# A macaron decoder trunk on one core: chunk of four feature tiles first, and the pair by seven block products, in feed-forwards 2 to 4

## The chip, the cores and the metric

One core of one Trainium2 chip runs the kernel. The metric is device microseconds of one execution; the time is the median of several. The engines: TensorE (PE) multiplies and transposes, VectorE (DVE), ScalarE (ACT) and GpSimd (POOL) work on elements, SyncE (SP) issues loads.

## The reference

Two layers on x of 512 tokens by 1024 features, float32. Each is a feed-forward, a token mixer and a feed-forward, all on a residual stream:

```python
def swiglu(x, w_in, w_out):
    g, u = jnp.split(x @ w_in, 2, axis=-1)
    return (jax.nn.silu(g) * u) @ w_out

for i in range(DEPTH):
    h = h + 0.5 * swiglu(rms_norm(h, ffn1_norm[i]), ffn1_w_in[i], ffn1_w_out[i])
    hn = rms_norm(h, mix_norm[i])
    # layer 0: a gated linear recurrence; layer 1: a chunked causal spatial gate
    h = h + mixer(hn)
    h = h + 0.5 * swiglu(rms_norm(h, ffn2_norm[i]), ffn2_w_in[i], ffn2_w_out[i])
return rms_norm(h, final_norm)
```

D_FF is 2816, so w_in is 1024 x 5632 and w_out 2816 x 1024. There are four feed-forwards; "feed-forward 1" to "4" below are these in order of time.

## The kernel before

**Numbers.** All large products are float32 by three matmuls: each operand is split into a high and a low part (`hi`, `lo`; for weights `whi`, `wlo`), and high x high, low x high and high x low are summed. ACT writes the high part by a copy, VectorE the low part by a subtraction. A weight tile holds 128 x 1024 numbers and is split whole.

**Seven products.** `seven` multiplies a 2 x 2 block matrix (two halves of the tokens by two halves of the contracted features) with a 2 x 2 block matrix of weights by seven block products in place of eight, in the order P1, P2, P5, P6, P3, P7, Q4. Their left operands are A11, A12, S1, S2, S4, S3 and A22, where S1 = A21 - A22, S2 = S1 - A11, S4 = S2 + A12 and S3 = -S2 - A22. The weight sums are made in place in the raw weight tile, either by VectorE (`raw<-raw,raw`) or by an accumulating load that POOL issues. `cuts` divides the contracted tiles of a half; with two cuts each product takes two steps.

**Feed-forward.** `FF_PARTS` divides the 22 feature tiles into three parts. Each part projects in, applies SiLU and the product, transposes the result into left operands, and projects out (`out_blocks`). Part one is a pair of feature tiles and a chunk of four; parts two and three are two chunks of four. A chunk is `chunk`: `seven` with 512 columns and two cuts, 14 steps of 12 matmuls. The pair is `pair_plain`: four weight tiles (gate and up columns side by side, 512 columns), used in six steps of 12, 12, 24, 24, 12 and 12 matmuls, with A12, then A11 and S1 together, then A22 against the summed weights.

**Order of the work.** `manual_schedule` keeps the order written. The list `subs` holds all steps. In iteration i of the main loop each engine's queue gets, in this order: the hooks "pre", a weight add for step i+4, the split of the weights of step i+3, the hooks "mid" and "rest", loads, the matmuls of step i with what reads their banks, the hooks "end" and "late". There are four buffers for each of `whi` and `wlo`, so step i+3 is split into the buffers of step i-1. There are eight raw buffers (`rawp`).

**The norm between stages.** `BlockNorm` turns the residual X into the left operands of the next stage while the out-projection before it still runs. `quarter` is called when a quarter of X is final; the last is A21, at step n of that out-projection, and `rest(n)` sets the later sums and splits relative to n: `s2` in step n+4+i for column group i, its split in n+5+i, `s4` and `s3` in steps n4 and n3, their splits one later. So the next stage's first step is n+1. The flag `plain` serves the spatial block, whose second half also reads A21 itself. `BlockNorm` is made at four places: after the recurrent block (for feed-forward 2), after feed-forward 2 (for 3), after feed-forward 3 (for the spatial block, with `plain`), and after the spatial block (for 4).

Of the kernel before, what the change touches and what calls it, by code (L numbers as in the profile page):

```python
# [13 lines left out]
P = 128  # L14
# [3 lines left out]
DFF = 2816  # L18
# [6 lines left out]
V_F1, V_MIX, V_F2, V_CW, V_CB, V_GA, V_GX, V_LAM, V_SB = 0, 16, 32, 48, 80, 88, 96, 104, 112  # L25
# [2 lines left out]


FF_PARTS = (("p", 4), (4, 4), (4, 4))  # L30

RAW_BUFS = 8
SPLIT_AHEAD = 3
# [19 lines left out]
def trunk(ctx: ExitStack, tc: tile.TileContext, a: dict, out: bass.AP):  # L53
# [57 lines left out]
    class Raw:  # L111
# [4 lines left out]
        def __init__(self, src, shape, plus=None):  # L116
            self.src, self.shape, self.plus, self.uses, self.done = src, shape, plus, 0, 0
# [87 lines left out]
    subs = []  # L205
    hooks = {}

    def hook(n, phase, fn):


        hooks.setdefault((n, phase), []).append(fn)
# [106 lines left out]
    def seven(block, cuts, left, w, posts, order=None, own=False, apart=False, joined=None):  # L318

        bk, raw, held = {}, {}, []
        banks = dict(BANK, Q4=("Q", True)) if apart else BANK

        def mm_of(prod, ci):
            name, fresh = banks[prod]
            pairs = cuts[ci]  # L330

            def mm(sub):
                if fresh and ci == 0:
                    for s in range(2):
                        bk[name, s] = bank(name)[:, :w]
                if prod == joined and ci == 0:
                    held.extend((sub, q, i) for q, i in enumerate(pairs))
                    return
                for s in range(2):
                    ps = bk[name, s]  # L340
                    k = {} if fresh else dict(skip_group_check=True)
                    for sb, q, i in (held if prod == joined else []) + [(sub, q, i) for q, i in enumerate(pairs)]:
                        zh, zl = left(prod, i, s)
                        wh, wl = sb.hi[:, q, :], sb.lo[:, q, :]
                        end = i == cuts[-1][-1]
                        nc.tensor.matmul(ps, zh, wh, start=fresh and i == 0, stop=False, **k)  # L346
                        nc.tensor.matmul(ps, zl, wh, start=False, stop=False, **k)  # L347
                        nc.tensor.matmul(ps, zh, wl, start=False, stop=end, **k)  # L348
                    if ci == len(cuts) - 1 and prod in posts:
                        posts[prod](s, ps)  # L350
            return mm

        order = order or [(p, ci) for p in ORDER for ci in range(len(cuts))]
        for prod, ci in order:
            def new(k, n, plus=None):
                b = lambda k, n: block(k, n, cuts[ci])
                return raw_of(b(k, n), [P, len(cuts[ci]), w], plus and b(*plus))

            tile = then = tile_then = None
            if prod == "P1":  # L360
                r = raw[11, ci] = new(0, 0)
            elif prod == "P2":
                r = new(1, 0)
            elif prod == "P5":
                if own:
                    raw[11, ci] = new(0, 0, (0, 1))
                    if joined:
                        then = block(1, 1, cuts[ci])
                else:
                    tile = raw[12, ci] = new(0, 1)  # L370
                    tile_then = block(1, 1, cuts[ci])
                r = raw[11, ci]
            elif prod == "P6" and joined:
                r, then = raw[11, ci], block(1, 0, cuts[ci])
            elif prod == "P6":
                r, tile, then = raw[11, ci], new(1, 1), block(1, 0, cuts[ci])
                raw[22, ci] = tile
            elif prod == "P3":
                r = new(1, 1) if joined else raw[22, ci]
            elif prod == "P7":  # L380
                r = new(0, 1, (1, 1)) if own else raw[12, ci]
            else:
                r = raw[11, ci]
            subs.append(Sub(r, mm_of(prod, ci), None, tile, then, tile_then))
        return order
# [49 lines left out]
    class BlockNorm:  # L435


        def __init__(self, grow, plain=False):
            self.g = [Group(2), Group(2)]
            self.grow, self.plain = grow, plain  # L440

        def src(self, i, name):
            t0, c = QUARTER[name]
# [13 lines left out]
        def rest(self, n, a22=4):  # L457

            for i, g in enumerate(self.g):
                if a22 is not None:  # L460
                    hook(n + (9 if self.plain else a22), "mid", lambda g=g: g.parts("A22"))
                hook(n + 4 + i, "pre", g.s2)
                hook(n + 5 + i, "mid", lambda g=g: g.parts("S2"))
                n4, n3 = (n + 6 + i, n + 8 + i) if self.plain else (n + 7 + 2 * i, n + 10 + i)
                hook(n4, "pre", g.s4)
                hook(n4 + 1, "mid", lambda g=g: g.parts("S4", True))
                if self.plain:
                    hook(n3, "pre", lambda g=g: tt(g.new("A21"), g.f["S1"], g.f["A22"], ALU.add))
                    hook(n3 + 2, "mid", lambda g=g: g.parts("A21", True))
                hook(n3, "pre", g.s3)  # L470
                hook(n3 + 1, "mid", lambda g=g: (g.parts("S3", True), g.f.pop("S2")))
                hook(n3 + 1, "late", lambda g=g: g.f.pop("A22"))
# [148 lines left out]
    def in_block(w, col, cw):  # L621

        def block(k, n, cut):
            r0 = k * 512 + cut[0] * P
            return w[r0 : r0 + len(cut) * P, col(n) : col(n) + cw].rearrange("(q p) c -> p q c", p=P)
        return block

    def x_left():
        return left_of(lambda: S.z)


    def chunk(w_in, f0, nt, group):

        w = nt * P
        c1, c2, c3, c5, ht = {}, {}, {}, {}, {}

        def rt(t):
            return S.rt[:, t : t + 1]

        def new(d, s, name):  # L640
            d[s] = slot(name=name)[:, :w]
            return d[s]

        def p1(s, ps):
            act(new(c1, s, "c1"), ps, AF.Copy)

        def p2(s, ps):
            tt(c1[s], c1[s], ps, ALU.add)
            hook(now[0] + 1, "mid", lambda: act(c1[s], c1[s], AF.Silu, scale=rt(s)))

        def p5(s, ps):
            act(new(c5, s, "c5"), ps, AF.Copy)

        def p6(s, ps):
            act(new(c2, s, "c2"), ps, AF.Copy)

        def p3(s, ps):
            tt(c2[s], ps, c2[s], ALU.subtract)
            stt(c2[s], c2[s], rt(s), c1[s], ALU.mult, ALU.mult)
            ht[s] = c2[s]  # L660
            if s == 1:
                left_blocks(group, ht, 0)

        def p7(s, ps):
            act(new(c3, s, "c3"), ps, AF.Copy)
            hook(now[0] + 1, "mid", lambda: tt(c5[s], c5[s], c3[s], ALU.subtract))

        def q4(s, ps):
            s4 = slot(name="s4")[:, :w]
            act(s4, ps, AF.Silu, scale=rt(2 + s))  # L670
            stt(c5[s], c5[s], rt(2 + s), s4, ALU.mult, ALU.mult)
            ht[2 + s] = c5[s]
            if s == 1:
                left_blocks(group, ht, 1)

        seven(in_block(w_in, lambda n: n * DFF + f0 * P, w), [[0, 1], [2, 3]], x_left(), w,
              dict(P1=p1, P2=p2, P5=p5, P6=p6, P3=p3, P7=p7, Q4=q4))

    def pair_plain(w_in, f0, group, first=False):
# [58 lines left out]

    def ffn(w_in, w_out, norm):
        f0 = 0  # L740
        for i, sizes in enumerate(FF_PARTS):
            groups, p0 = [], f0
            for n in sizes:
                if n == "p":
                    groups.append(Group(1))
                    pair_plain(w_in, f0, groups[-1], not subs)
                    f0 += 2
                else:
                    groups.append(Group(n // 2))
                    chunk(w_in, f0, n, groups[-1])  # L750
                    f0 += n
            gs = out_blocks(w_out, p0, [g.n for g in groups], 0.5, norm if i == len(FF_PARTS) - 1 else None, own=True)
            gs.update(enumerate(groups))
# [533 lines left out]

    last = FinalNorm()
    ffn(a["ffn1_w_in"][0], a["ffn1_w_out"][0], TileNorm(V_MIX))
    recurrent(a["rec_w_in"][0], a["rec_w_out"][0], BlockNorm(V_F2))  # L1290
    ffn(a["ffn2_w_in"][0], a["ffn2_w_out"][0], BlockNorm(V_F1 + 8))
    ffn(a["ffn1_w_in"][1], a["ffn1_w_out"][1], BlockNorm(V_MIX + 8, True))
    spatial(a["sg_w_in"][0], a["sg_w_out"][0], BlockNorm(V_F2 + 8))
    ffn(a["ffn2_w_in"][1], a["ffn2_w_out"][1], last)
    hook(len(subs) - 24, "late", last.load)
    hook(len(subs) - 16, "rest", last.halve)
# [152 lines left out]
```

## Time and profile before

| | |
|---|---|
| median of 3 runs | 1651.8 us (1651.05 to 1652.23) |
| profiled execution, its span | 1651.2 us, 20805 instructions |
| granted TensorE clock, mean | 0.997 |
| loaded from memory | 269.55 MB, 165 GB/s over the span |

The page times one execution; its span is from the first instruction to the last. A group row gives the line, engine, operation, operands by name (buffer numbers left out) and shape, the count, then busy time and mean ns of one, then idle time of the engine just before and what ended it. A waits row gives who waited for whom: total us, times, longest. A timeline row gives start, duration, engine, line, operation, operands, and in brackets an idle time ahead of it with its releaser. A windows row gives a stretch, its length, then busy us and instructions of PE, PEld (weight load), DVE, ACT and POOL (or of those asked for), then the granted clock, DMA share and GB/s. Names: `p` are the pair's banks, A, B, C, Q those of `seven`, `r` the recurrent projection's, `a` and `s` hold left operands, `c` the chunk's results, `e` transposes.

### The profile page before, as it was taken

What the parts mean: (1) busy time and instruction counts of PE and PEld (TensorE: products, weight loads), DVE (VectorE), ACT (ScalarE), POOL (GpSimd) and SP (SyncE); (2) the same over time, 40 slices, a digit from 0 to 9 for tenths busy, and PEclk for the clock granted to TensorE, in tenths of its full rate; (3) what the DMA queues carried; (4) which work ended last, traced back from release to release, by engine and by line L of the source; (5) the groups of instructions that cost most, each with busy time, mean ns of one, the idle gap of its engine ahead of it and who ended that gap; (6) DMA issues with size and microseconds to landing.
All of it is one profiled execution on the core that took longest, in us unless ns stands there. A gap on an engine that the chain in (4) does not pass through costs nothing. (4 is left out here: it accounts for less than half of the span.)

```text
span 1651.2 us, 20805 instructions
## 1 busy us (share of the span) xinstructions
PE 1621.7 (98%) x7475; PEld 1333.0 (81%) x7475; DVE 1369.8 (83%) x1814; ACT 1035.8 (63%) x1490; POOL 212.3 (13%) x193
## 2 busy tenths in 40 slices
PE   8999999989999999999999999999999999999997
PEld 6788888878878888888888888888888888888885
DVE  5898897787798897878988978878966988879777
ACT  6656656666957656556676565566864765665655
POOL 1111111200010111111101111111100011121120
PEclk9999999999999999999999999999999999999999
DMA  6767876952463876876838778768863557686693
GB/s 205 159 171 176 209 163 153 219 141 77 102 153 92 189 169 162 218 177 157 202 95 181 176 162 209 184 163 204 216 169 90 151 122 186 166 208 169 157 230 79
DMA packets 161288, 273.02 MB, mean 165 GB/s; under 512 B 11312, under 2 KB 37536, under 8 KB 161184
## 3 DMA queue, kind: packets, MB, share of 16 engines
q1 hardware_dynamic: 113856, 182.74, 35.9%
q0 software_dynamic: 45536, 87.10, 31.4%
q10 hardware_dynamic: 1792, 1.84, 0.4%
q8 instruction: 59, 0.97, 0.2%
q14 instruction: 45, 0.37, 0.1%
HBM read 269.55 MB, written 2.10 MB: 165 GB/s over the span
## 5 line engine op out<-in xcount | busy, mean ns | idle before, releaser
L96 ACT ACTIVATE whi<-raw 128x1024 fp32r<-128x1024 f32 (+1 forms) x539 | 556.4, 1034 | 423.0 <-PE A L347 108.2
L87 DVE TENSOR_TENSOR wlo<-raw,whi 128x1024 fp32r<-128x1024 f32 (+1 forms) x539 | 641.0, 1192 | 203.7 <-ACT whi L96 202.8
L346 PE MATMUL A<-whi,hi 128*128 128x512 f32 x984 | 393.1, 399 | 4.3 <-DVE x L93 4.3
L347 PE MATMUL A<-whi,lo 128*128 128x512 f32 x984 | 386.2, 392 | 3.6 <-DVE lo L87 3.5
L348 PE MATMUL A<-wlo,hi 128*128 128x512 f32 x984 | 385.7, 392 | 0.2 <-DVE wlo L87 0.2
L347 PEld LDWEIGHTS A<-whi,lo 128*128 128x128 f32 x984 | 185.7, 189 | 43.8 <-DVE lo L87 7.1
L346 PEld LDWEIGHTS A<-whi,hi 128*128 128x128 f32 x984 | 185.5, 189 | 41.2 <-issue 4.7
L348 PEld LDWEIGHTS A<-wlo,hi 128*128 128x128 f32 x984 | 185.6, 189 | 40.8 <-DVE wlo L87 0.6
L347 PE MATMUL C<-whi,lo 128*128 128x512 f32 x544 | 212.4, 390 | 0.9 <-DVE lo L87 0.7
L346 PE MATMUL C<-whi,hi 128*128 128x512 f32 x544 | 212.4, 390 | 0.0
L348 PE MATMUL C<-wlo,hi 128*128 128x512 f32 x544 | 211.8, 389 | 0.0
L136 POOL DMA_DIRECT2D raw<-in_ffn_w_in_dram x80 | 96.4, 1205 | 757.3 <-DVE raw L87 551.8
L87 DVE TENSOR_TENSOR raw<-raw,raw 128x1024 f32<-128x1024 f32 (+1 forms) x116 | 139.1, 1200 | 0.5
L87 DVE TENSOR_TENSOR lo<-a,hi 128x512 fp32r<-128x512 f32 (+1 forms) x196 | 127.9, 659 | 11.5 <-ACT hi L96 11.1
L136 POOL DMA_DIRECT2D raw<-in_ffn_w_out_dram x74 | 85.5, 1162 | 382.8 <-DVE wlo L87 128.1
L96 ACT ACTIVATE hi<-a 128x512 fp32r<-128x512 f32 (+1 forms) x196 | 117.5, 601 | 8.4 <-DVE a L87 6.1
L347 PEld LDWEIGHTS C<-whi,lo 128*128 128x128 f32 x544 | 102.1, 188 | 24.2 <-DVE lo L87 3.3
L346 PEld LDWEIGHTS C<-whi,hi 128*128 128x128 f32 x544 | 102.1, 188 | 21.5 <-ACT c L96 0.4
L348 PEld LDWEIGHTS C<-wlo,hi 128*128 128x128 f32 x544 | 102.1, 188 | 21.1
L96 ACT ACTIVATE c<-A 128x512 f32<-128x512 f32 x126 | 74.1, 595 | 56.9 <-PE A L348 56.5
L346 PE MATMUL B<-whi,hi 128*128 128x512 f32 x272 | 109.1, 401 | 0.0
L348 PE MATMUL B<-wlo,hi 128*128 128x512 f32 x272 | 106.2, 391 | 0.0
(169 smaller groups left out, 2182.3 us busy)
## 6 DMA issues: line engine op xcount, KB each, us to landing
raw<-in_ffn_w_in_dram SPq DMA_DIRECT2D x160, 512.0 KB, 4.4
raw<-in_ffn_w_out_dram SPq DMA_DIRECT2D x100, 512.0 KB, 5.4
raw<-in_ffn_w_in_dram POOLq DMA_DIRECT2D x80, 512.0 KB, 7.6
raw<-in_ffn_w_out_dram POOLq DMA_DIRECT2D x62, 512.0 KB, 8.3
raw<-in_sg_w_in_dram SPq DMA_DIRECT2D x18, 512.0 KB, 5.1
raw<-in_rec_w_in_dram SPq DMA_DIRECT2D x16, 512.0 KB, 3.8
raw<-in_ffn_w_in_dram SPq DMA_DIRECT2D x30, 256.0 KB, 3.6
raw<-in_ffn_w_out_dram SPq DMA_DIRECT2D x20, 256.0 KB, 4.5
```

Of the source, the lines that this page charges most:

```text
L87: nc.vector.tensor_tensor(out=o, in0=x, in1=y, op=op)
L96: nc.scalar.activation(out=o, in_=x, func=f, **k)
L136: nc.gpsimd.dma_start(out=self.v, in_=src, accum_op=ALU.add)
L346: nc.tensor.matmul(ps, zh, wh, start=fresh and i == 0, stop=False, **k)
L347: nc.tensor.matmul(ps, zl, wh, start=False, stop=False, **k)
L348: nc.tensor.matmul(ps, zh, wl, start=False, stop=end, **k)
```

## The change

Feed-forwards 2 to 4 take `LATER_PARTS`: in part one the chunk of four tiles comes first and the pair second, and the pair is now `chunk` with two feature tiles: `seven` with 256 columns and one cut of four contracted tiles, seven steps of 24 matmuls. Feed-forward 1 keeps its parts. `BlockNorm` gets a flag `block`, which is set for the norms ahead of feed-forwards 2, 3 and 4 and, through `plain or block`, for the one ahead of the spatial block. The times of S4 and S3 that went by `plain` go by `block`, and so does the late split of A22, which now comes in n+9 for the first column group and n+10 for the second, in place of n+9 for both. `plain` alone still decides whether A21 itself is made.

```diff
+LATER_PARTS = ((4, 2), (4, 4), (4, 4))
...
-        def __init__(self, grow, plain=False):
+        def __init__(self, grow, plain=False, block=False):
             self.g = [Group(2), Group(2)]
-            self.grow, self.plain = grow, plain
+            self.grow, self.plain, self.block = grow, plain, plain or block
...
             for i, g in enumerate(self.g):
                 if a22 is not None:
-                    hook(n + (9 if self.plain else a22), "mid", lambda g=g: g.parts("A22"))
+                    hook(n + (9 + i if self.block else a22), "mid", lambda g=g: g.parts("A22"))
                 hook(n + 4 + i, "pre", g.s2)
                 hook(n + 5 + i, "mid", lambda g=g: g.parts("S2"))
-                n4, n3 = (n + 6 + i, n + 8 + i) if self.plain else (n + 7 + 2 * i, n + 10 + i)
+                n4, n3 = (n + 6 + i, n + 8 + i) if self.block else (n + 7 + 2 * i, n + 10 + i)
                 hook(n4, "pre", g.s4)
                 hook(n4 + 1, "mid", lambda g=g: g.parts("S4", True))
                 if self.plain:
...
-        seven(in_block(w_in, lambda n: n * DFF + f0 * P, w), [[0, 1], [2, 3]], x_left(), w,
+        cuts = [[0, 1], [2, 3]] if nt == 4 else [[0, 1, 2, 3]]
+        seven(in_block(w_in, lambda n: n * DFF + f0 * P, w), cuts, x_left(), w,
...
-        for i, sizes in enumerate(FF_PARTS):
+        for i, sizes in enumerate(FF_PARTS if not subs else LATER_PARTS):
...
-    recurrent(a["rec_w_in"][0], a["rec_w_out"][0], BlockNorm(V_F2))
-    ffn(a["ffn2_w_in"][0], a["ffn2_w_out"][0], BlockNorm(V_F1 + 8))
+    recurrent(a["rec_w_in"][0], a["rec_w_out"][0], BlockNorm(V_F2, block=True))
+    ffn(a["ffn2_w_in"][0], a["ffn2_w_out"][0], BlockNorm(V_F1 + 8, block=True))
     ffn(a["ffn1_w_in"][1], a["ffn1_w_out"][1], BlockNorm(V_MIX + 8, True))
-    spatial(a["sg_w_in"][0], a["sg_w_out"][0], BlockNorm(V_F2 + 8))
+    spatial(a["sg_w_in"][0], a["sg_w_out"][0], BlockNorm(V_F2 + 8, block=True))
```

## The prediction

> **What bounds the kernel now.** I read the page's engine table first, then TensorE's timeline, the busy time of each engine by stage, and the waits.
>
> ```profile
> PE 1621.7 (98%) x7475; PEld 1333.0 (81%) x7475; DVE 1369.8 (83%) x1814; ACT 1035.8 (63%) x1490; POOL 212.3 (13%) x193
> ```
>
> TensorE (PE) is the bound and VectorE (DVE) is next. PE's 98% is no price, because matmuls overlap; what one costs is read from start to start.
>
> ```profile
> 850.53 0.39 PE L700 MATMUL p<-whi,hi 128*128 128x512 f32 x1
> ...
> 855.97 0.39 PE L700 MATMUL p<-whi,hi 128*128 128x512 f32 x1
> ...
> 367.03 0.28 PE L219 MATMUL r<-zl,whi 128*128 128x256 f32 x1
> ...
> 374.23 0.28 PE L219 MATMUL r<-zl,whi 128*128 128x256 f32 x1
> ```
>
> The first two rows are 24 matmuls of 512 columns apart (the pair's fourth step): 5.44/24 = 0.227 us each. The other two are 60 matmuls of 256 columns apart (recurrent projection): 7.20/60 = 0.120 us. A step (one `Sub`: one product on one weight tile) of 12 wide matmuls is therefore 2.72 us.
>
> ```profile
> 506.01:529.04 23.03, 23.03 (x109) 18.98 (x108) 18.45 (x32) 15.22 (x24) 0.00 (x0) 1.00 0.29 92
> 529.04:569.03 39.99, 39.99 (x186) 32.92 (x184) 34.61 (x47) 26.79 (x40) 6.92 (x6) 1.00 0.76 163
> 569.03:599.29 30.26, 30.09 (x136) 24.27 (x134) 28.75 (x43) 17.26 (x26) 4.21 (x4) 1.00 0.77 202
> ```
>
> These are windows over feed-forward 2's pair, its chunk and its first out-projection: length, then busy PE, weight load, DVE, ACT, POOL. Together 93.3 us, of which VectorE works 18.45 + 34.61 + 28.75 = 81.8. It is hidden, but barely: 4.6, 5.4 and 1.5 us are spare.
>
> ```profile
> ACT whi L96 <- PE A L347: 108.2, 92, 1.9
> DVE wlo L87 <- ACT whi L96: 202.8, 171, 5.0
> PE A L347 <- DVE lo L87: 3.5, 3, 2.2
> ```
>
> The waits show the loop: ACT's weight split waits for PE (four split buffers, split three steps ahead, so the split for step k+3 starts when step k-1 ends), VectorE follows ACT, and PE hardly ever waits for a split operand.
>
> **The change part by part.**
>
> *Pair, PE.* Plain accumulation is 96 matmuls of 512 columns: 96 x 0.227 = 21.8 us. Seven products are 7 x 24 = 168 of 256: 168 x 0.120 = 20.2 us. That saves 1.6 us in each of three feed-forwards, **-4.8**. It is time of the bound itself, so it counts whole. The transposes stay the same in number. Bounds: -7.7 and +30, from the two rivals on spacing below; the 60-matmul row is the very shape with its weight loads, so I take it.
>
> *Chunk first: what is late next.* The pair asked for S1 in its third step; now S1 is read in step 5, a slack that buys nothing. S2, read in step 7 (P6, first cut), is next. Counted from the stage's first step, `block` puts S2's sums in steps 4 and 5 and its splits in 5 and 6 (as before), S4's splits in 7 and 8, S3's in 9 and 10, A22's in 9 and 10.
>
> ```profile
> 838.53:861.56 23.03, 22.64 (x96) 17.77 (x96) 0.88 (x3) 1.31 (x3) 1.00 0.29 92
> ...
> 849.36 0.68 DVE L87 TENSOR_TENSOR a<-s,a 128x512 f32<-128x512 f32 x1
> ...
> 516.86 0.68 DVE L87 TENSOR_TENSOR a<-s,a 128x512 f32<-128x512 f32 x1
> ...
> 1318.49 0.68 DVE L87 TENSOR_TENSOR a<-s,a 128x512 f32<-128x512 f32 x1
> ```
>
> The window is feed-forward 3's pair alone, 96 matmuls from 838.53. The sum of S2 starts 10.8 us into it, and likewise 10.85 after the 506.01 of the window of feed-forward 2; feed-forward 4 has its own at 1318.49. Ahead of it VectorE already does the adds for steps 5 and 6. What the items cost there, from start to start, shows in a stretch of the spatial in-projection, which works in this same order:
>
> ```profile
> 1182.89 1.22 DVE L87 TENSOR_TENSOR raw<-raw,raw 128x1024 f32<-128x1024 f32 x1
> 1184.02 1.22 DVE L87 TENSOR_TENSOR wlo<-raw,whi 128x1024 fp32r<-128x1024 f32 x1
> 1185.16 1.28 DVE L87 TENSOR_TENSOR c<-c,B 128x512 f32<-128x512 f32 x2
> 1186.35 0.68 DVE L87 TENSOR_TENSOR a<-s,a 128x512 f32<-128x512 f32 x1
> 1186.96 1.22 DVE L87 TENSOR_TENSOR wlo<-raw,whi 128x1024 fp32r<-128x1024 f32 x1
> 1188.09 0.68 DVE L87 TENSOR_TENSOR lo<-a,hi 128x512 fp32r<-128x512 f32 x1
> ...
> 1188.47 0.39 PE L346 MATMUL A<-whi,hi 128*128 128x512 f32 x1
> 1188.83 0.50 PE L347 MATMUL A<-whi,lo 128*128 128x512 f32 x1
> ```
>
> VectorE has no gap here: an add takes 1.13, a wlo 1.14, a 512-wide item 0.60. S2's lo, from 1188.09, makes step 7's second matmul start 0.36 after the first in place of 0.23: 0.13 late. The chunk in feed-forward 3 has step 7's add (1.13) ahead of 849.36's work, which then starts at 850.5. From there to the end of its lo stand the sum 0.60, step 8's add 1.13, wlo 1.14, P2's two adds 1.19, the other group's sum 0.61, wlo 1.13 and lo 0.68: 857.0. Step 7 begins 72 wide matmuls into the stage; the old fourth step began after 48 (12 + 12 + 24), so step 7 stands at the second fence's 855.97, and its second matmul at 856.2. It waits 0.8: **+2.5** in three feed-forwards. Bounds: 0.4 (the recorded 0.13 three times) and 6 (2.0 each: the two adds before S2 as well). The count of items speaks for 0.8.
>
> S4 is then in time: after 857.0 come a sum, wlo, lo, sum, wlo and lo, 4.8 us, so 861.8 against step 9's second matmul at 855.97 + 0.8 + 5.44 + 0.23 = 862.4. S3 and A22 have more. Cover for all of these is VectorE's lead; if it is gone, each late split costs what it is late.
>
> *Pair, the other engines.*
>
> ```profile
> L93 DVE SCALAR_TENSOR_TENSOR h<-p,rt,s 128x256 f32<-128x256 f32 x16 | 7.3, 480 | 2.1 <-ACT s L96 1.8
> L87 DVE TENSOR_TENSOR lo<-a,hi 128x256 fp32r<-128x256 f32 x20 | 8.4, 419 | 0.0
> L96 ACT ACTIVATE s<-p,rt 128x256 f32<-128x256 f32 x16 | 7.1, 475 | 2.7 <-PE p L702 2.7
> raw<-in_ffn_w_in_dram POOLq DMA_DIRECT2D x80, 512.0 KB, 7.6
> ACT whi L96 <- DMA raw<-in_ffn_w_out_dram: 5.3, 3, 3.7
> ```
>
> VectorE gets a seventh split (1.22) and six more 256-wide adds and subtractions (6 x 0.42); the four scaled products of 0.48 stay four, the two weight adds stay two. That is 3.7 us, 85.5 against some 92: hidden, with no room for a second such addition. ACT gets one split and eight copies of some 0.4, about 4 us, and has more than 30 spare. SP's loads stay four blocks, in half as many transfers; the chunk's eight loads and four POOL additions now go ahead of them and use the same eight buffers, which the out-projection before has given back. POOL gets two more accumulating loads per feed-forward, on a queue that is busy 13%.
>
> The second of them is the one to watch. It follows P6's low part, and Q4's split reads it. From 857.0 VectorE's queue up to that low part holds ten wlo, two adds, 17 items of 0.60 and four of 0.68, 26.6 us: 883.6. PE starts the pair at 855.97 + 0.8 + 8 x 2.72 = 878.5, so the load is issued about 5 us in and lands 7.6 later, at 12.7. ACT wants to split Q4 when P5 ends, 3 x 24 x 0.120 = 8.6 in: it stands 4 us there. Behind it in its queue are P6's copies, done by 12.7 + 1.1 + 0.8 = 14.6; P7 needs them at 5 x 2.88 = 14.4. Two sets of transposes lie in between and give PE about a microsecond, so I take 0; bounds 0 and 2 each (landing at 10). The last row shows that such a stand of ACT exists (3.7 us).
>
> *Out-projection.* The order of its two cuts turns round. Nine 0.60 items of the chunk's sums leave it for the pair's stage or stay (four), and nine of the half-width ones come: the same within half a microsecond of VectorE. Taken as 0, bounds -0.5 and +0.5 each.
>
> *Spatial norm.* It is made with `plain`, and `block` follows it, so its times stay, but for the second A22 split, one step later (step 10) and read in step 14: hidden by four steps, 0.
>
> Sum: -4.8 + 2.5 = -2.3 on the profiled 1651.2, 1648.9; the median of the runs is 0.6 above that execution, so **1649.5**.
>
> **Rivals.**
> *Faster, S2 in time.* if the new add falls into idle time of VectorE, the wait stays at 0.13: 1651.8 - 4.8 + 0.4 = 1647.4.
>
> ```profile
> 842.03 0.88 DVE L93 SCALAR_TENSOR_TENSOR s<-e,vec,a 128x256 f32<-128x256 f32 x2 [0.69 <-PE e L260]
> ```
>
> For it: these 0.69 us, and 4.6 spare in the old pair. Against it: the add for step 7 stands in the queue behind this row (two steps on), and the old order shows no other idle time up to 849.36.
>
> *Slower, the accumulating load.* If it lands 10 us or more after its issue, ACT's copies hold up P7 by 2 us or more in each pair: 1649.5 + 6 = 1655.5 and up. It decides from a landing of about 8.5 on. For it: rows of 1 KB in place of 2 KB, twice as many pieces; against it: the median of 7.6 is from stretches with two such loads at once.
>
> *Slower, VectorE as the bound.* Each feed-forward loses 2 us more than taken, also 1655.5: the 93% become more where the queue holds a stretch of 26.6 us against 21.8 of PE (8 x 2.72). Against it: the pair gives it back.
>
> *Spacing.* A 512-column matmul takes 0.107 us more than one of 256, so 0.013 of each is fixed. Were it hidden, the pair would save 96 x 0.213 - 168 x 0.107 = 2.5 us: 1651.8 - 7.7 + 2.5 = 1646.6. The trace's 60 matmuls speak against it. The Trainium skill ("TensorE: Matmul & The Clock Gate", Back-to-back issue gap) has N/2.4 + 2.5 ns for a lone stream, 216 and 109 ns, close to this case; the trace's spacings are 5 and 10% longer and decide.
>
> *Weight loads.*
>
> ```profile
> L347 PEld LDWEIGHTS A<-whi,lo 128*128 128x128 f32 x984 | 185.7, 189 | 43.8 <-DVE lo L87 7.1
> ```
>
> Were a 256-column matmul too short to hide the next weight load of 0.189, a pair would be 168 x 0.189 = 31.8, 10 more: 1651.8 + 30 + 2.5 = 1684. The 0.120 with a load for each speaks against it. The same page (What overlaps and what doesn't) lets a weight load overlap running matmuls only in another row group; the trace does not agree.
>
> **How the numbers follow.** Forecast 0.53 (1648.5 to 1651.5 on its own); S2 in time 0.29; accumulating load 0.08; VectorE 0.05; spacing 0.03; weight loads 0.02. A difference under 0.2%, 3.3 us, a measurement of this kernel can't tell from none, so no change is 1648.5 to 1655.1. Faster is 0.29 + 0.03 and 0.03 of the forecast's lower edge, 0.35; slower is 0.08 + 0.05 + 0.02 less 0.04 that would end under 1655.1, 0.11; the rest 0.54. The range goes from 1647 to 1655.
>
> **What would show it.** The three pairs at 20 to 22 us with their transposes in place of 23.0, 168 matmuls 0.120 apart; one wait of PE for `lo` of about 0.8 at the first P6 step of the chunk in feed-forwards 2 to 4; ACT standing some 4 us at the pair's Q4 split, with no gap on PE; the spatial stage unchanged. The forecast is wrong if that wait is missing (then 1647) or if PE stands at P7 or Q4 of the pair.

## The result and the profile after

| | before | after |
|---|---|---|
| median of 6 runs | 1652.36 us (1651.05 to 1653.19) | 1655.68 us (1653.75 to 1658.78) |
| profiled execution, span | 1651.2 us | 1653.4 us (time 1655.38) |

The ratio of the runs is 1.0026, with a 95% interval of 1.0016 to 1.0036 (of the two medians alone, 1.0020). The change costs about 3 us where a gain of 2.3 was forecast; the time lies above the range. The engine table of the page, after the change:

```profile
PE 1618.4 (98%) x7691; PEld 1341.0 (81%) x7691; DVE 1378.6 (83%) x1835; ACT 1045.0 (63%) x1517; POOL 220.0 (13%) x199
```

TensorE has less busy time than before (1621.7) and the kernel takes longer: PE did save work, and stood more. The windows of feed-forward 2's part one, in the new order chunk, pair, first out-projection (columns as in the windows of before):

```profile
505.39:548.31 42.92, 40.91 (x188) 33.06 (x186) 41.23 (x59) 32.38 (x48) 6.11 (x5) 1.00 0.63 143
548.31:570.67 22.36, 21.76 (x181) 21.40 (x180) 16.45 (x25) 12.84 (x23) 3.95 (x4) 1.00 0.74 173
570.67:599.86 29.19, 29.19 (x133) 24.09 (x132) 27.43 (x45) 17.03 (x28) 3.63 (x4) 1.00 0.77 198
```

Compare stage by stage. The chunk goes from 39.99 to 42.92, the pair from 23.03 to 22.36, the out-projection from 30.26 to 29.19: 93.3 becomes 94.5. Feed-forwards 3 and 4 give 94.08 and 94.72. That is 1.16 more on the mean, 3.5 in three, and no other stage took part: the spatial in-projection went from 41.09 to 41.04, the recurrent out-projection from 45.49 to 45.46. The two spans are 2.2 apart, since what lies ahead of the recurrent out-projection and what lies behind feed-forward 4's part one, which the change leaves alone, were each 0.6 shorter in this execution. In the chunk VectorE is busy 41.23 of 42.92, where it was 34.61 of 39.99: the norm's work on S1, S2 and the splits of A22, which used to lie beside the pair, now lies beside the chunk, where the sums of S4 and S3 already were.

PE's waits over that same part one:

```profile
PE e L261 <- DVE c L94: 1.8, 3, 1.0
PE A L348 <- DVE lo L88: 0.7, 1, 0.7
```

Before, this view has no wait of PE in that stretch. The second row is the one that was forecast, for S2. The first, more than twice as large, was not: `e` are banks of transposes, `c` the results of chunk and pair. Below, main matmuls are those of the products, and PE stands where it runs none of them. PE's timeline in feed-forward 3 shows where each stands. First step 7, then the end of step 11 (P7, first cut):

```profile
856.54 0.39 PE L347 MATMUL A<-whi,hi 128*128 128x512 f32 x1
857.60 0.50 PE L348 MATMUL A<-whi,lo 128*128 128x512 f32 x1 [0.68 <-DVE lo L88]
...
870.90 0.39 PE L349 MATMUL A<-wlo,hi 128*128 128x512 f32 x1
871.62 0.30 PE L261 MATMUL e<-ident,c 128*128 128x128 f32 x1 [0.34 <-DVE c L94]
872.92 0.55 PE L261 MATMUL e<-ident,c 128*128 128x128 f32 x3 [1.00 <-DVE c L94]
873.22 0.48 PE L347 MATMUL A<-whi,hi 128*128 128x512 f32 x1
```

In step 7 the second matmul starts 1.06 after the first in place of 0.23. Behind step 11, 2.32 us pass from the last main matmul to the next; four transposes of the chunk's first results stand in PE's own queue there, ahead of step 12's matmuls, and VectorE hasn't made those results yet. VectorE's timeline:

```profile
856.87 0.68 DVE L88 TENSOR_TENSOR lo<-a,hi 128x512 fp32r<-128x512 f32 x1
...
870.01 0.68 DVE L88 TENSOR_TENSOR c<-C,c 128x512 f32<-128x512 f32 x1
870.73 0.75 DVE L94 SCALAR_TENSOR_TENSOR c<-c,rt,c 128x512 f32<-128x512 f32 x1
871.40 0.68 DVE L88 TENSOR_TENSOR c<-C,c 128x512 f32<-128x512 f32 x1
872.12 0.75 DVE L94 SCALAR_TENSOR_TENSOR c<-c,rt,c 128x512 f32<-128x512 f32 x1
```

No row carries a bracket, and neither does any left out between them: VectorE isn't waiting, it works through its queue without a gap. P3's two products (the `c<-c,rt,c` rows) end at 871.48 and 872.87, and PE's transposes start 0.14 and 0.05 after that.

The pair, in the same feed-forward: ACT, then VectorE, then PE.

```profile
894.96 1.06 ACT L97 ACTIVATE whi<-raw 128x1024 fp32r<-128x1024 f32 x1 [2.86 <-DMA raw<-in_ffn_w_in_dram]
```

```profile
896.05 1.22 DVE L88 TENSOR_TENSOR wlo<-raw,whi 128x1024 fp32r<-128x1024 f32 x1 [3.78 <-ACT whi L97]
```

```profile
897.27 0.28 PE L347 MATMUL A<-whi,hi 128*128 128x256 f32 x1
...
900.03 0.28 PE L349 MATMUL A<-wlo,hi 128*128 128x256 f32 x1
...
900.77 0.33 PE L261 MATMUL e<-ident,c 128*128 128x128 f32 x1 [0.35 <-DVE c L94]
900.86 0.36 PE L347 MATMUL A<-whi,hi 128*128 128x256 f32 x1
```

ACT stands 2.86 for the accumulating load of Q4's weights, VectorE 3.78 behind ACT, and again it is at the transposes behind P7 that PE waits. The 24 matmuls of P7 are 2.76 us apart from the first to the last, 23 spacings: 0.120 each, as forecast.

So what one part one gained and lost, as the mean of three:

| item | us |
|---|---|
| pair's matmuls, as forecast (with no wait 21.37, see e4_q4_vector, against 23.03) | -1.66 |
| wait for S2 in step 7 (step of 3.71 in place of 2.72) | +0.99 |
| chunk's transposes behind step 11 (step of 4.82; 3.08 where they don't wait) | +1.74 |
| rest of the chunk | +0.19 |
| pair's late load and its transposes (22.29 against 21.37) | +0.92 |
| out-projection (29.22 against 30.26) | -1.04 |
| sum | +1.14 |

### The profile page after: what moved, and what is told of

The parts are those of the page before. It is cut to its first block, busy times and chain, and to the rows that moved or that the text cites. A ratio compares the mean times of both kernels' runs of the same rounds, so it can differ in the third digit from the quotient of the medians.

```text
span 1653.4 us, 21285 instructions
## 1 busy us (share of the span) xinstructions
PE 1618.4 (98%) x7691; PEld 1341.0 (81%) x7691; DVE 1378.6 (83%) x1835; ACT 1045.0 (63%) x1517; POOL 220.0 (13%) x199
## 5 line engine op out<-in xcount | busy, mean ns | idle before, releaser
L347 PE MATMUL A<-whi,hi 128*128 128x512 f32 (+1 forms) x1080 | 420.8, 390 | 4.2 <-DVE x L94 4.2
L348 PE MATMUL A<-whi,lo 128*128 128x512 f32 (+1 forms) x1080 | 413.4, 383 | 5.7 <-DVE lo L88 5.6
L349 PE MATMUL A<-wlo,hi 128*128 128x512 f32 (+1 forms) x1080 | 412.9, 382 | 0.2 <-DVE wlo L88 0.2
L347 PEld LDWEIGHTS A<-whi,hi 128*128 128x128 f32 x1080 | 204.4, 189 | 41.1 <-issue 4.6
L348 PE MATMUL C<-whi,lo 128*128 128x512 f32 (+1 forms) x592 | 225.6, 381 | 0.7 <-DVE lo L88 0.7
L347 PE MATMUL C<-whi,hi 128*128 128x512 f32 (+1 forms) x592 | 226.2, 382 | 0.0
L349 PE MATMUL C<-wlo,hi 128*128 128x512 f32 (+1 forms) x592 | 225.4, 381 | 0.0
L97 ACT ACTIVATE c<-A 128x512 f32<-128x512 f32 (+1 forms) x144 | 79.9, 567 | 57.1 <-PE A L349 56.5
L347 PE MATMUL B<-whi,hi 128*128 128x512 f32 (+1 forms) x296 | 115.8, 391 | 0.0
L349 PE MATMUL B<-wlo,hi 128*128 128x512 f32 (+1 forms) x296 | 112.9, 381 | 0.0
```

Of the source, the lines that this page charges most:

```text
L97: nc.scalar.activation(out=o, in_=x, func=f, **k)
```

## The experiments

All are edits of the changed kernel. The theory is that VectorE has one queue, which runs late by the norm's work that moved beside the chunk, and that PE meets this debt at two places (S2's split in step 7, the transposes behind step 11), and the pair's load at a third. The rivals are that the order costs nothing and the seven products cost it, or that S2's wait causes the later one.

**The order alone: e1_order_only.** The chunk first, but the pair by plain accumulation again.

```diff
-LATER_PARTS = ((4, 2), (4, 4), (4, 4))
+LATER_PARTS = ((4, "p"), (4, 4), (4, 4))
```

> Order alone: chunk first, but the pair by plain accumulation (96 matmuls of 512 columns). Theory (the order costs, the seven products pay): the chunk-first stage keeps its 42.9 us with the same two waits (S2's lo at step 7, 0.9; the transposes behind step 11 waiting for P3's products, 1.7), the pair is back at 23 us or a little more, so part one is about 95.8 us against 93.3 before and 94.1 to 94.7 with the change: about 1659.5 us in all, slower than the change by some 4 and than before by some 7. Rival (the seven products cost more than they save, through their added loads and vector work): the kernel is no slower than the change, 1655 us or less.

Measured: 1658.88 us against 1651.7 of before, ratio 1.0040 (1.0027 to 1.0053). Its windows of chunk and pair in feed-forward 2:

```profile
506.45:549.35 42.90, 40.88 (x187) 33.07 (x186) 40.08 (x58) 32.37 (x48) 4.81 (x4) 1.00 0.57 135
549.35:572.25 22.90, 22.90 (x108) 18.89 (x106) 14.72 (x19) 9.06 (x12) 4.20 (x4) 1.00 0.59 145
```

The chunk has the same 42.90 with a plain pair behind it, and the pair is 22.90, close to the 23.03 of before. Part one is 95.25 (before 93.28): the order costs 2.0 in each feed-forward, the seven products give back 0.8 of it as built, and 1.8 where their load isn't late (e4_q4_vector, 93.47). The loss belongs to the order. The out-projection is 29.45 here, so 0.8 of its 1.04 comes with the order too.

**The transposes one step later: e2_transposes_later.** In the first chunk of feed-forwards 2 to 4 the transposes of the first half are queued one step later. They are wanted in the out-projection only.

```diff
-                left_blocks(group, ht, 0)
+                left_blocks(group, ht, 0, lag)
...
-                    chunk(w_in, f0, n, groups[-1])
+                    chunk(w_in, f0, n, groups[-1], 2 if sizes == (4, 2) and n == 4 else 1)
```

> The change with the transposes of the first chunk's A11 and A12 each one step later (behind steps 12 and 13 in place of 11 and 12). Theory (TensorE stands behind step 11 because the transposes in its queue need P3's products, which VectorE reaches late): that 1.7 us goes from each of three feed-forwards, the chunk-first stage is 41.2 us in place of 42.9, about 1650.5 us in all. Rival (VectorE is simply the bound of the stage, so the wait turns up at a later step): the stages together stay within 0.5 us, 1655 us.

Measured: 1650.74 us, ratio 0.9991 (0.9982 to 1.0000). The chunk's window, and PE's only wait in it:

```profile
506.39:547.60 41.21, 40.51 (x188) 33.11 (x186) 40.44 (x57) 32.15 (x48) 6.11 (x5) 1.00 0.63 146
```

```profile
PE A L348 <- DVE lo L88: 0.7, 1, 0.7
```

41.21, 41.22 and 41.17 in the three feed-forwards, 1.7 less in each. The wait for S2 stays, the wait of the transposes is gone, and no other takes its place. VectorE's work is the same, 40.44 busy of 41.21; it was PE's queue that turned its lateness into a stand.

**S2's split earlier: e3_s2_early.** S2's split goes ahead of the splits of the weights in its iteration.

```diff
-                hook(n + 5 + i, "mid", lambda g=g: g.parts("S2"))
+                hook(n + 5 + i, "pre" if self.block and not self.plain else "mid", lambda g=g: g.parts("S2"))
```

> The change with S2's split ahead of the weight split of the same iteration in ACT's and VectorE's queues. Theory (one VectorE backlog, two places where TensorE meets it): the 0.94 us at step 7 goes, but TensorE comes to the transposes behind step 11 that much earlier and waits there 2.6 in place of 1.7; the chunk-first stage stays at 42.9 us, 1655 to 1656 us in all. Rival (the two waits are separate): the stage is 42.0 us, about 1653 us.

Measured: 1656.87 us, ratio 1.0033 (1.0022 to 1.0044). The wait in step 7 is gone, and the chunk got longer, 44.23 on the mean, which neither theory nor rival had expected. PE's timeline behind step 11, and the windows of the chunk and of the 3.4 us that follow the stand:

```profile
870.95 0.39 PE L349 MATMUL A<-wlo,hi 128*128 128x512 f32 x1
872.21 0.30 PE L261 MATMUL e<-ident,c 128*128 128x128 f32 x1 [0.87 <-DVE c L94]
873.51 0.55 PE L261 MATMUL e<-ident,c 128*128 128x128 f32 x3 [1.00 <-DVE c L94]
873.81 0.48 PE L347 MATMUL A<-whi,hi 128*128 128x512 f32 x1
```

```profile
839.92:884.15 44.23, 42.37 (x188) 34.21 (x186) 40.74 (x58) 32.32 (x48) 6.11 (x5) 0.96 0.65 151
...
873.81:877.22 3.41, 3.41 (x13) 2.71 (x12) 3.41 (x4) 1.83 (x3) 0.00 (x0) 0.62 0.30 82
```

Of the 0.99 that PE no longer waits in step 7, 0.22 comes back in step 9 and 0.54 in step 11: the first transpose waits 0.87 in place of 0.34, since PE came there 0.8 earlier and VectorE only 0.2. This is the debt of one queue, met at later places. Behind the stand, 2.86 us from one main matmul to the next, the granted clock then fell for some 3.4 us, in which 13 matmuls ran where the changed kernel runs 20 (below). Step 12 is 1.57 longer by that, more than the wait that was saved; without it the chunk would be some 42.7, an estimate from these steps, near the 42.9 that the theory gave. The profiled execution, 1658.66 us, is the longest of its seven; whether the clock falls three times in the others isn't shown.

**The pair's load: e4_q4_vector.** Q4's weights are summed by VectorE from a block already there, in place of the second accumulating load.

```diff
-                r = new(1, 0)
+                r = raw[21, ci] = new(1, 0)
...
                 raw[22, ci] = tile
+                if len(cuts) == 1:
+                    then = None
...
                 r = raw[11, ci]
+                if len(cuts) == 1:
+                    tile = raw[21, ci]
```

> The change with the pair's Q4 weights summed by VectorE from P2's raw tile, which stays loaded, in place of POOL's accumulating load. Theory (that load lands late, ACT stands at the Q4 split, VectorE stands behind ACT, P3's products of the pair come late and TensorE's transposes behind P7 wait 0.5 to 1.1 us): that wait goes, the pair's stages are about 21.4 us in place of 22.4, 21.9 and 22.6, about 1653.3 us in all, against 1.1 us more vector work for each pair. Rival (the wait behind P7 comes from VectorE's own amount of work): it grows, pairs of 22.5 to 23.5 us, 1656 to 1658 us.

Measured: 1650.44 us, ratio 0.9994 (0.9984 to 1.0004). The pair's window in feed-forward 2:

```profile
546.68:568.05 21.37, 21.37 (x181) 21.36 (x180) 17.25 (x25) 12.94 (x23) 2.09 (x2) 1.00 0.58 152
```

21.37 in all three, PE without a gap. VectorE has 0.8 more to do than in the changed kernel's pair, and still isn't late: the load was what was late, not VectorE's work. The stages explain 2.9 us of the 5.2 by which the median lies below that of the changed kernel. The rest stays open; the two come from different sets of runs, in which the medians of before are 0.7 apart.

**Both of the chunk's waits: e6_two.** The edits of e2_transposes_later and e3_s2_early together.

> The change with both edits of the chunk-first stage: the first chunk's A11 and A12 transposes one step later, and S2's split ahead of the weight split. Theory (both waits are one VectorE backlog, which ends on its own by step 13, so TensorE loses nothing once nothing it needs stands behind that backlog; and without the long stand the granted clock stays up): the stage is 40.3 us in place of 42.9, no half-clock stretch behind step 11, about 1648 us in all. Rival (the backlog comes out at a third place): the stage stays at 41.2, 1650.7 us as with the transposes alone.

Measured: 1649.97 us, ratio 0.9984 (0.9975 to 0.9994). The chunk in feed-forward 3:

```profile
838.98:879.40 40.42, 40.42 (x188) 33.12 (x186) 39.45 (x56) 32.09 (x48) 6.11 (x5) 1.00 0.64 146
```

PE is busy all of its 40.42. With the transposes out of the way S2's early split pays 0.8 more than e2_transposes_later; alone it cost 1.3, the fallen clock included. The same edit has two signs, by what is next in PE's queue. The median is 2 us above the 1648 that was expected. Half of that stands in the pair, which is 22.64 on the mean in place of 22.29, or 1.0 in three: PE comes to it earlier, and in feed-forward 3 its transposes wait 0.9 there, against 0.35 in the changed kernel.

**All three: e5_all3.** The edits of e2, e3 and e4 together.

> The two edits of the chunk-first stage and the pair's Q4 weights summed by VectorE, all at once. Theory (three separate places, the savings add): stage 40.3, pairs 21.4, out-projection 29.2, part one 90.9 us against 93.3 before; about 1645.5 us in all, which is faster than before by 0.35%. Rival (VectorE, with 1.1 us more for each pair and less waiting of TensorE to hide in, is the bound now): pairs of 22.5 us or more, 1648 to 1650 us.

Measured: 1644.58 us against 1652.58, ratio 0.9954 (0.9942 to 0.9965). Its part one in feed-forward 2:

```profile
504.72:545.15 40.43, 40.43 (x187) 33.11 (x186) 39.77 (x57) 32.10 (x48) 6.11 (x5) 1.00 0.62 145
545.15:566.52 21.37, 21.37 (x181) 21.37 (x180) 18.36 (x26) 12.61 (x23) 2.09 (x2) 1.00 0.67 161
566.52:595.69 29.17, 29.17 (x133) 24.09 (x132) 27.57 (x46) 17.03 (x28) 4.24 (x4) 1.00 0.81 204
```

The savings add: 90.97 in place of 94.47, and PE's busy time equals the length in each row. Against before it is 2.3 a feed-forward, 6.9 in three; the medians are 8.0 apart. This version beats both kernels.

**The same stand in feed-forward 1: e7_all3_ff1.** e5_all3, with the later transposes in feed-forward 1's chunk as well, which the change doesn't touch.

```diff
-                    chunk(w_in, f0, n, groups[-1], 2 if sizes == (4, 2) and n == 4 else 1)
+                    chunk(w_in, f0, n, groups[-1], 2 if i == 0 and n == 4 else 1)
```

> As the kernel with all three edits, and feed-forward 1's chunk too has its A11 and A12 transposes one step later. Theory (the kernel before already has the same stand at that place, 69.8 to 72.7 us, and the half-clock stretch at 73 to 76 us follows from it): the chunk of feed-forward 1 takes 42.7 us in place of 46.0, of which 1.7 is the stand and 1.6 the clock; about 1642 to 1643 us in all. Rival (the half-clock stretch near 74 has another cause): 44.3 us, 1644 us.

Measured: 1643.59 us, ratio 0.9942 (0.9930 to 0.9954). Feed-forward 1's chunk in before, here, and in e5_all3:

```profile
37.05:83.07 46.02, 43.28 (x186) 33.81 (x184) 40.78 (x59) 31.24 (x48) 7.85 (x7) 0.96 0.69 147
```

```profile
36.84:78.95 42.11, 41.29 (x185) 32.73 (x184) 40.61 (x59) 31.20 (x48) 6.96 (x6) 1.00 0.64 140
```

```profile
37.38:81.82 44.44, 41.64 (x186) 32.67 (x184) 40.77 (x59) 31.24 (x48) 6.96 (x6) 1.00 0.70 145
```

The chunk is 3.9 shorter than in before, and its clock 1.00 in place of 0.96. But e5_all3's chunk has the same stand (2.90 us from main matmul to main matmul) and its clock is 1.00 all the same, so against its profile the saving is 2.3: the edit takes away the stand, and the 1.6 of the clock only in executions that lose it. The recorded rival, that the half-clock stretch has another cause, isn't excluded by this run. The median is 1.0 below e5_all3's, and the two intervals overlap: the stage's saving is shown, the kernel's is not.

**VectorE with less to do: e8_no_adds.** P5's two weight sums are not made in the first chunk of feed-forwards 2 to 4.

```diff
+        if drop:
+            subs[at + 4].skip = subs[at + 5].skip = True
```

> The change with the two weight sums for steps 5 and 6 of the first chunk (P5's) left out in feed-forwards 2 to 4, so P5's weights are wrong there; 2.27 us less vector work ahead of both waits, nothing moved. Theory (one VectorE backlog): the wait at step 7 is nil, and the one of the transposes behind step 11 is 1.7 + 0.9 - 2.3 = 0.4 us: the stage is 40.6 us, about 1649 us in all. Rival (the transposes wait for something else than VectorE's backlog, their own products' chain): the stage is 42.0 us, 1653 us.

Measured: 1653.27 us, ratio 1.0006 (0.9997 to 1.0016), and the chunk 42.20 on the mean. The theory's 40.6 missed; the rival's 42.0 is near. In feed-forward 3:

```profile
838.59:880.79 42.20, 40.87 (x187) 33.09 (x186) 38.85 (x56) 32.36 (x48) 3.70 (x3) 1.00 0.50 122
```

```profile
855.65 0.69 DVE L88 TENSOR_TENSOR lo<-a,hi 128x512 fp32r<-128x512 f32 x1
...
868.79 0.69 DVE L88 TENSOR_TENSOR c<-C,c 128x512 f32<-128x512 f32 x1
```

```profile
866.96 0.39 PE L351 MATMUL C<-wlo,hi 128*128 128x512 f32 x1
```

VectorE was spared two adds, 2.27 by the 1.13 of each, but S2's low part came only 0.7 earlier (17.06 into the stage in place of 17.77): that far ahead VectorE still stands idle for PE's transposes of A21, and the adds had partly filled that. The wait in step 7 fell from 0.99 to 0.28; the step with the transposes stayed at 4.82, since PE and VectorE both came 0.7 earlier. The stage's length doesn't tell theory and rival apart, but the rows do. The rival was that the transposes wait for their own products' chain; yet the last matmul of P3 starts at 866.96 and VectorE takes up P3's products at 868.79, with no gap in its queue from 850 on. The products wait for their turn in VectorE's queue, and e3_s2_early agrees, since there the debt showed at later places.

## Why the prediction was wrong, point by point

**The step that failed** is in "Chunk first: what is late next". It followed VectorE's queue item by item, but asked only when the split operands of the main matmuls come (S2, S4, S3, A22), and so put the chunk's own transposes at nothing, without a reason. "The transposes stay the same in number", under "Pair, PE", is true of the number and says nothing of what they wait for. The working wrote down that VectorE's queue holds a stretch of 26.6 us against 21.8 of PE, and didn't ask what else of PE's queue reads from that stretch. The chunk's products do; the transposes that read them stand in order between step 11 and step 12. That is +1.74 in each feed-forward, +5.2: more than the pair's whole gain of 4.8. With it on its own the forecast would have been 1654.7.

**The accumulating load** was the second failure, of place more than of size. The load was taken to land 12.7 into the pair; ACT went on 12.95 into it (894.96 less 882.01). The near hit has some luck in it: counted from the stage's start, the pair began 2.9 later than reckoned and P6's low part ended 3.0 later. ACT's stand was put at 4 and is 2.86. But the working looked for the damage at P6's copies, which hold nothing up, and missed that VectorE stands behind ACT's split with P3's products behind that (3.78), and PE's transposes behind those. The cost taken was 0; it is 0.92 in each, +2.8. The text itself named a stand of PE at the pair's P7 or Q4 as a sign that it is wrong, and there it is, right behind P7.

**S2's wait** was right: forecast 0.8, measured 0.83 as the forecast counted it (1.06 less 0.23, at the second matmul) and 0.99 over the whole step. The items summed to a low part that starts 17.79 into the stage (857.0 less 0.68, from 838.53); it started 17.77 in. **S4, S3 and A22** were in time: the view of waits has no row for them. **The pair on PE** was right: 0.120 a matmul, 21.37 without the late load. **The out-projection** was taken as 0 within 0.5 and gave 1.04 in each, -3.1; e1_order_only puts most of it down to the order, and PE's rows in feed-forward 2 show where it lies. The first two steps are 0.55 and 0.12 shorter: each has two transposes of the pair in place of four of the chunk, which now stand in the pair's window. Step 7 is 2.72 in place of 3.08; in before its second matmul, at 588.49, started behind a low part that VectorE ended at 588.43. **The spatial stage** stayed, as forecast. The working also set the span of 1651.2 against the median of the times, as if the two were one measure; after the change the time is 2.0 above the span. The error cancels, since the sum was in the end taken from the median.

From -2.3 to the measured +3.5 in the stages: transposes +5.2, late load +2.8, S2 +0.5, the chunk's rest +0.6, out-projection -3.1, pair's spacing -0.2, rounding aside.

**Of the rivals**, "VectorE as the bound" gave 1655.5 and a chance of 0.05, against which the text put that the pair gives the debt back. It can't: PE has stood by then, and TensorE's lost time doesn't come back. What it lacked was the place where PE meets the debt. The rival of the accumulating load also gave 1655.5, by another way: a landing of 8.5 us or more that holds up P7. The median landing was 7.4, and P7 wasn't held up. The sign of what did happen was in the profile of before. Feed-forward 1 has its pair first, in a stage with a late VectorE, and PE's timeline shows this very stand there, behind P7's first cut:

```profile
69.81 0.39 PE L348 MATMUL A<-wlo,hi 128*128 128x512 f32 x1
71.10 0.30 PE L260 MATMUL e<-ident,c 128*128 128x128 f32 x1 [0.91 <-DVE c L93]
72.40 0.55 PE L260 MATMUL e<-ident,c 128*128 128x128 f32 x3 [1.00 <-DVE c L93]
72.71 0.48 PE L346 MATMUL A<-whi,hi 128*128 128x512 f32 x1
```

The chunks of feed-forwards 2 to 4 had no such row. Their VectorE was busy 34.61 of 39.99, that of feed-forward 1 40.61 of 42.11 once the stand is gone (e7_all3_ff1); that this slack is the reason is argued. A change that takes the slack away should have been priced with this stand as a bound: 2.9 us, and 1.6 more where the clock falls behind it.

## What to carry to other kernels

When work is moved beside a stage, follow the busier engine's queue item by item, as here, but then list everything on the bounding engine that reads from it: its transposes stand in order between the main matmuls, and one of them that waits holds up all behind it. If the value isn't wanted soon, queue its reader a step later; that cost nothing here and took away 1.7 us a stage. A wait that is removed upstream only helps when nothing downstream waits for the same queue: the same edit cost 1.3 us alone, through the clock, and paid 0.8 behind the other.

## What the runs showed of the hardware

**The granted clock can fall behind a short stand.** These windows of 3.4 us each begin with the first main matmul behind a stand at the transposes: in feed-forward 1 of before and of e5_all3 (PE alone), and in feed-forward 3 of the changed kernel:

```profile
72.71:76.12 3.41, 3.41 (x13) 0.63 0.84 156
```

```profile
73.03:76.44 3.41, 3.41 (x20) 1.00 0.89 171
```

```profile
873.22:876.60 3.38, 3.38 (x20) 2.81 (x19) 3.38 (x4) 2.15 (x4) 0.00 (x0) 1.00 0.28 82
```

A fourth is e3_s2_early's above. After 2.90 us from main matmul to main matmul (before) and 2.86 (e3_s2_early) the clock is some 0.62 and 13 matmuls run; after 2.32 us it is 1.00 and 20 run. Seven matmuls of 0.227 make 1.6 us for each such event. The four transposes in between didn't keep the clock up. In e3_s2_early it happened in feed-forwards 2 to 4 alike, in those of the changed kernel in none.

The length alone doesn't decide. Feed-forward 1 has a stand of 2.85 to 2.90 us in eight of the ten profiles; the clock fell behind it in before, the changed kernel, e3_s2_early and e8_no_adds, and stayed at 1.00 in e1_order_only, e2_transposes_later, e4_q4_vector and e5_all3. What tells these apart is not shown.

The Trainium skill ("TensorE: Matmul & The Clock Gate", HAM oscillation and Part 4) has idle gaps of more than about 3.4 us as the cause, and says that a transpose doesn't count as PE-busy in the same way. The four transposes that didn't keep the clock up are in line with the second. The first is not what the runs show: 2.9 us were enough in some executions and not in others.

**Executions of one kernel differ, and the longer ones tend to have the lower clock.** In e6_two's twelve runs the time goes from 1645.08, at a mean granted clock of 0.998, to 1652.26 at 0.995; the shortest of the changed kernel and its longest, 1653.75 and 1658.78, have 0.997 and 0.994. Half-clock stretches come at the same places in one profile and not in another, as in these 10 us of the recurrent part, which no edit touches, in the changed kernel and in e6_two:

```profile
460.00:470.00 10.00, 7.84 (x35) 6.25 (x34) 10.00 (x19) 4.83 (x7) 1.20 (x1) 1.00 0.88 186
```

```profile
460.00:470.00 10.00, 7.82 (x28) 6.00 (x27) 9.97 (x20) 4.60 (x7) 1.61 (x2) 0.83 0.84 160
```

So where a stage's length in the profile resolves a microsecond, the medians don't always.
